# Four adaLN units per layer summed by TensorE in the router's span, branch and out products in another order without GpSimd, and the overfull-expert branch in the last expert pair

## The chip, the cores and the metric

The kernel runs on one core of a Trainium2 chip. The metric is the device time of one execution in microseconds (us). Besides TensorE (PE; its weight loads are listed as PEld) the core has VectorE (DVE), ScalarE (ACT), GpSimd (POOL) and SyncE (SP), which here issues the loads of weights; 16 DMA engines carry them.

## The reference

Two layers work on 256 tokens of width 1024. Six vectors per layer ("sections") come from one product with the conditioning vector c (adaLN): shift, scale and gate for the mixer and for the experts.

```python
c_act = jax.nn.silu(c)
for l in range(DEPTH):                              # 2
    mod = c_act @ ada_w[l] + ada_b[l]               # ada_w[l]: 1024 x 6144
    sh1, sc1, g1 = ...                              # sections 0, 1, 2
    sh2, sc2, g2 = ...                              # sections 3, 4, 5
    h = rmsnorm(x, norm1_g[l]) * (1.0 + sc1) + sh1
    x = x + g1 * token_mix(h, ...)
    h = rmsnorm(x, norm2_g[l]) * (1.0 + sc2) + sh2
    x = x + g2 * grouped_moe(h, w_router, router_bias, w_gate[l], w_up[l], w_down[l])
return rmsnorm(x, final_g)

# token_mix, its end:
    o_a = rmsnorm(o_a, hg_norm_g) * jax.nn.silu(hgate)
    merged = sigmoid(gates_a) * (o_a @ w_br_a) + sigmoid(gates_b) * (o_b @ w_br_b)
    return merged @ w_out

# grouped_moe: 16 experts of width 512, the best 2 of one group of 4 for each token
    he = jax.nn.silu(t @ w_gate[e]) * (t @ w_up[e])
    y = y + combine[:, e:e + 1] * (he @ w_down[e])
```

## The kernel before

Activations stand transposed (128 channels by 256 tokens, 8 such blocks). Every product of the mixer splits its fp32 weights into a high and a low part: `wunit` casts a 128x512 block on ACT and subtracts on DVE (both L409), into a ring of four buffers, and PE then makes 12 matmuls of 128x256 from it (L551). The sections of the input projection come in the order lat, qf, vg, ga, gb; then attention and the recurrence; then the branch products ("br", w_br_a and w_br_b) and the product with w_out ("out"). In `br` there are four steps i, each with a pair of output blocks: two units with the attention result `ob` make `gb`, two with the recurrence's result (`oah`, `oal`, which lie in buffers attn and vm) make `ga`, each multiplied on DVE (L909); GpSimd (for i < 3) then adds them to `m` (L913) and subtracts for the low part `hB` of the merged value, ACT casts the high part `hA`. `out` then takes its units one block of 128 columns after another, each over both halves of `hA` and `hB`.

`chain()` normalises the heads of the recurrence: four reciprocals (L884), two scaled copies (L886), a product with the output gate on GpSimd (L889) and a split with the subtraction on GpSimd. It is run a step at a time by `tick()`, which `wunit` calls: every unit advances each generator in the list `aside` by one.

adaLN: the first two sections of layer 0 are summed by PE at the start (`ada_sum`, L356: 8 matmuls of 128x256 with 32 columns of weights for a unit, a quarter of a section; the profile shows each as two; ACT copies the bank, L360; `ada_finish` adds four row groups by matmuls with one column and the bias on DVE). All other sections are summed by a custom reduction on DVE, two instructions of 128x1024 for a unit (`ada_steps`, L376, shown as CUSTOM_DVE_ANT_0). These are spread by `tick()` too, one instruction in 2 units of the mixer in layer 0, in 3 in layer 1: layer 0 has six sections (24 units), layer 1 four (16 units). What is left when the heads are done is run after the gates (layer 1) and after `br` (`while aside: tick()`).

The experts: tokens are sorted into 64 slots per expert by one-hot matrices. `moe()` makes the router's products (L979, L181), chooses on DVE (up to `selb`, L1026), ranks by a matmul with the triangle `tri`, gathers the tokens of four experts (L181, then L1103 and L1105), and runs the experts in eight pairs: gate and up (L1112), `he` (L1178), four transposes (L1187), a copy `heT` (L1189), down (L1121), and a scatter-add. `overflow()` holds a conditional block (`tc.If`, L1144, on a count that every engine's sequencer loads, L1141) for experts with over 64 tokens; it is placed between the first gather and the first pair. In these runs the block is not entered.

The order on each engine is the program's. SP's queue issues all weight loads (`fetch`, L190) in one order, each waiting until its buffer is free. The buffers A0, A1, B0, B1, C0, C1, x0, x1 hold 2 MB, r0, r1, hA, hB, n8, o9 1 MB, vm and attn 0.5 MB; several hold an activation in one phase and a weight in another. `early` and `late` load pieces of the first pairs' weights into activation buffers that have become free, `latest` one more (n8) behind the conditional block.

Of the kernel before, what the change touches and what calls it, by code (L numbers as in the profile page):

```python
# [19 lines left out]
P = 128  # L20
# [47 lines left out]
N_MSK = P * (len(LEVELS) + 2)  # L68
SECTIONS = ("qf", "vg", "ga", "gb", "br", "out")
# [31 lines left out]
def _lay_out(v):  # L101
# [31 lines left out]
    ada = _rows(w[:1, :, :2 * D]).reshape(P, J, 8, QD)  # L133
    ada = np.moveaxis(ada, 2, 0).reshape(2, 4, P, QUART)
# [21 lines left out]
def trunk(ctx: ExitStack, tc: tile.TileContext, x, pos, vec_in, msk_in, lat_in, wb, wq_in, wkv_in, ada_in, adat_in, crow_in, we,  # L156
# [72 lines left out]
    ada_at = {0: [(0, 2), (0, 3), (0, 4), (0, 5), (1, 0), (1, 1)], 1: [(1, 2), (1, 3), (1, 4), (1, 5)]}  # L229
# [6 lines left out]
    def issue():  # L236
        while todo and not todo[0]:
            todo.pop(0)
        for n, part in enumerate(todo[:2]):
            while part:  # L240
                key = part[0]
                if key[0] == "sec":
                    tags = ("A0", "A1", "B0") if key[2] in ("lat", "qf") else ("A0", "A1")
                elif key[1] > layer[0] or n and todo[0] and (todo[0][0][0] == "moe" or todo[0][0][2] in ("lat", "qf")):
                    break
                else:
                    tags = ("B0", "B1", "C0", "C1", "x0", "x1") + (() if n and todo[0] else ("A0", "A1"))
                s = [t for t in tags if t in free and t not in blocked]
                if not s:
                    break  # L250
                part.pop(0)
                if key[0] == "sec":
                    _, l, name, h = key
                    fetch(key, s[0], lat_in[l, h] if name == "lat" else wb[l, SECTIONS.index(name), h],
                          cuts=4 if key == ("sec", 1, "lat", 0) else 1)
                    if key == ("sec", 0, "lat", 0):
                        first_load(2)
                else:
                    _, l, p, i, h = key
                    fetch(key[:4], s[0], we[l, p, i][:, h * HALF:(h + 1) * HALF], h * HALF,  # L260
                          cuts=(1 if p < E // 2 - 1 else 4 if (i, h) in ((1, 1), (2, 1)) else 2))
# [9 lines left out]
    def early(l):  # L271
        at = HALF
        for t in ("vm", "attn", "r1"):
# [3 lines left out]

    def late(l):
        free.add("hA")
        fetch(("moe", l, 1, 1), "hA", we[l, 1, 1][:, HALF:HALF + QUART], HALF)  # L280

    def latest(l):
        at = HALF + QUART
        fetch(("moe", l, 1, 1), "n8", we[l, 1, 1][:, at:at + QUART], at)
# [8 lines left out]
    again, used_up = {}, {}  # L293
# [58 lines left out]
    def ada_sum(l, s, q, w, part):  # L352
        b = bank()
        for j in range(J):
            g = 32 * (j % 4)
            op = pe.matmul(b[g:g + 32, :QD], ca[:, j:j + 1].to_broadcast([P, 32]), w[:, j * QD:(j + 1) * QD],  # L356
                           start=j < 4, stop=j >= 4, tile_position=(0, g))
            if j == 0:
                tc.keep_in_program_order(op)
        ac.copy(part, b[:, :QD])  # L360
# [118 lines left out]
    def mixer(l, hs, after):  # L479
# [130 lines left out]
        aside.append(ada_steps(ada_at[l], 6, 2 if l == 0 else 3))  # L610
# [250 lines left out]
        disown("x0")  # L861
# [15 lines left out]
        def chain():  # L877
            yield
            for i, b in enumerate(ob_):
# [14 lines left out]
        aside.append(chain())  # L894
# [5 lines left out]
        while len(aside) > 1 or aside and l:  # L900
            tick()
        disown("C0")
        mg = [solo(t, [P, J, T], F32R) for t in ("hA", "hB")]
        w = section(l, "br")
        for i in range(4):
            js = slice(2 * i, 2 * i + 2)
            for g, ks, o in ((gb, 4, (ob[:, 0], ob[:, 1])), (ga, 0, (oah, oal))):
                b = pair(w, 256 * i, o, ks=(ks,), kx=ks)
                ve.scalar_tensor_tensor(g[:, js, :], g[:, js, :], 1.0, b.rearrange("p (h t) -> p h t", h=2),  # L909
                                        op0=ALU.add, op1=ALU.mult)  # L910
            m = t2("m")
            eng = gp if i < 3 else ve
            eng.tensor_tensor(m, gb[:, js, :], ga[:, js, :], ALU.add)  # L913
            split(mg[0][:, js, :], mg[1][:, js, :], m, eng)
            if i % 2:
                done("sec", l, "br", i // 2)
        disown("C1")
        while aside:
            tick()
        early(l)  # L920
# [5 lines left out]
        for i in range(4):  # L926
            b = pair(w, 256 * i, mg)
            for h in range(2):
                j = 2 * i + h
                ve.scalar_tensor_tensor(xT[:, j, :], b[:, h * T:(h + 1) * T], hg1[:, j:j + 1],  # L930
                                        xT[:, j, :], op0=ALU.mult, op1=ALU.add)
            if i % 2:
                done("sec", l, "out", i // 2)
            if i in (1, 2):
                next(after)
        disown("x1")
        late(l)

    def moe(l):
# [28 lines left out]
        for i in range(2):  # L968
# [15 lines left out]
            if i == 0:  # L984
                yield
        ve.tensor_reduce(rt, ssq, axis=AX.X, op=ALU.add)
# [12 lines left out]
        for (t, i), b in bx.items():  # L999
            ac.activation(hth[:, t, 4 * i:4 * i + 4, :], b.rearrange("p (q d) -> p q d", q=4), AF.Copy, scale=rv[:, t:t + 1])  # L1000
        bi = sm(TE, "bi")
# [159 lines left out]
        gather(oh, (2, 3))  # L1161
        weights(0, oh)
        overflow()
        latest(l)
        for p in range(E // 2):
# [6 lines left out]
            if last:  # L1172
                scatter(p - 1)
# [15 lines left out]
            ac.copy(heT, b.rearrange("p (j s) -> p j s", j=FJ))  # L1189
            if p and not last:  # L1190
# [121 lines left out]
```

## Time and profile before

| | |
|---|---|
| median of 3 runs | 987.47 us (983.97, 988.82, 987.47) |
| profiled execution | 983.23 us, span 981.4 us, mean granted clock 0.963 |
| busy: PE, DVE, ACT, POOL | 893.2 us (91%), 524.3 (53%), 340.5 (35%), 51.9 (5%) |
| DMA | 316.71 MB, mean 323 GB/s |
| L551, matmuls with hA (1312 of them) | 242.8 us, 16.1 us idle before them |
| layer 0: mixer to the end of the out product | 0 to 274 us |
| layer 0: router and experts | 274 to 506 us |
| layer 1: mixer | 506 to 737 us |
| layer 1: router and experts, then the final norm | 737 to 981.4 us |

The profile lists one execution. Busy time is that of an engine's own work; an idle time stands with the instruction that ended it, and with what released it ("<-"). PEclk is the granted share of TensorE's full clock. The stages in the last rows are read off the timeline of PE.

### The profile page before, as it was taken

How to read it: one execution, taken by the hardware profiler on the slowest of the kernel's cores; microseconds unless marked ns; L12 is line 12 of the kernel's file. 1: busy time of each engine (PE TensorE's matmuls, PEld its weight loads, DVE VectorE, ACT ScalarE, POOL GpSimd, SP SyncE). 2: the span in 40 equal slices, each digit the busy share in tenths (PEclk: the TensorE clock that was granted, in tenths of full speed). 3: DMA queues.
4: the chain of work that ended last, by engine and by line, in shares of the span. 5: the costliest groups of instructions: out<-in, count | busy, mean ns of one | idle time of the engine just before them, and what ended most of it. 6: DMA issues, size and time to landing. Idle time of an engine off the chain costs nothing. (4 is left out here: it accounts for less than half of the span.)

```text
span 981.4 us, 14762 instructions
## 1 busy us (share of the span) xinstructions
PE 893.2 (91%) x5958; PEld 635.6 (65%) x5958; DVE 524.3 (53%) x972; ACT 340.5 (35%) x632; POOL 51.9 (5%) x42
## 2 busy tenths in 40 slices
PE   5899999967969999999979999997895999999995
PEld 3688999957953535344349989997894353535333
DVE  4469898998540322222256968979854122322224
ACT  5465564524340212111146646554434111111103
POOL 0001100023000000000000020002300000000002
PEclk9899999998879999999999999999997999999998
DMA  9996665977659899999978626686585979999991
GB/s 362 430 378 225 234 224 217 380 307 315 253 210 381 344 384 430 434 427 429 422 299 329 271 91 248 253 326 250 224 348 200 398 306 433 429 429 433 426 386 43
DMA packets 35648, 316.71 MB, mean 323 GB/s; under 512 B 3952, under 2 KB 4208, under 8 KB 13808
## 3 DMA queue, kind: packets, MB, share of 16 engines
q1 hardware_dynamic: 35568, 315.64, 79.5%
q8 instruction: 50, 0.82, 0.3%
q14 instruction: 30, 0.25, 0.1%
HBM read 314.58 MB, written 1.05 MB: 322 GB/s over the span
## 5 line engine op out<-in xcount | busy, mean ns | idle before, releaser
L551 PE MATMUL bank<-hA,x 128*128 128x256 f32 x1312 | 242.8, 286 | 16.1 <-ACT x L409 8.8
L551 PEld LDWEIGHTS bank<-hA,x 128*128 128x128 f32 x1312 | 205.5, 192 | 20.3 <-DVE x L409 9.9
L551 PE MATMUL bank<-hB,x 128*128 128x256 f32 x656 | 184.7, 282 | 0.0
L551 PEld LDWEIGHTS bank<-hB,x 128*128 128x128 f32 x656 | 125.9, 192 | 0.2
L1178 DVE TENSOR_TENSOR he<-bank,sg 128x512 f32<-128x512 f32 x16 | 11.1, 692 | 141.8 <-PE bank L1112 113.4
L1137 DVE SCALAR_TENSOR_TENSOR xT<-bank,mod,xT 128x256 f32<-128x256 f32 x128 | 52.9, 478 | 58.1 <-PE bank L181 58.1
L1197 DVE SCALAR_TENSOR_TENSOR r<-bank,small,r 128x512 fp32r<-128x512 f32 (+1 forms) x36 | 24.7, 691 | 95.1 <-ACT r L1196 95.1
L1196 ACT ACTIVATE r<-bank,small 128x512 fp32r<-128x512 f32 (+1 forms) x36 | 22.8, 638 | 103.4 <-PE bank L1121 103.2
L1112 PE MATMUL bank<-moe_0B,o 128*64 128x512 f32 x192 | 47.6, 645 | 6.0 <-DVEq L1144 3.4
L1170 ACT ACTIVATE sg<-bank 128x512 f32<-128x512 f32 x16 | 9.6, 597 | 111.6 <-PE bank L1112 111.6
L1112 PE MATMUL bank<-moe_1x,o 128*64 128x512 f32 x192 | 43.4, 593 | 0.0
L1103 ACT ACTIVATE o<-bank,mod,acol 128x256 f32<-128x256 f32 x32 | 18.1, 564 | 58.5 <-DVE o L1105 55.0
L1189 ACT COPY heT<-bank 128x512 f32<-128x512 f32 x16 | 9.4, 588 | 83.4 <-PE bank L1187 83.4
L1112 PEld LDWEIGHTS bank<-moe_0B,o 128*64 128x64 f32 x192 | 15.2, 148 | 33.1 <-issue 32.6
L1112 PE MATMUL bank<-moe_1C,o 128*64 128x512 f32 x160 | 36.1, 592 | 0.0
L1105 DVE TENSOR_SCALAR o<-bank,acol,mod 128x256 f32<-128x256 f32 x32 | 17.4, 544 | 31.1 <-PE bank L181 28.2
L551 PE MATMUL bank<-o,x 128*128 128x256 f32 x192 | 28.1, 304 | 6.4 <-ACT x L409 3.4
L551 PE MATMUL bank<-attn,x 128*128 128x256 f32 x128 | 26.6, 300 | 6.4 <-DVE x L409 5.0
L1121 PE MATMUL bank<-moe_2C,heT 128*64 128x512 f32 (+1 forms) x160 | 29.2, 511 | 2.7 <-ACT heT L1189 2.7
L697 POOL TENSOR_TENSOR x<-ra,rbt 32x512 f32<-32x512 f32 x8 | 12.9, 1613 | 354.0 <-DVE rbt L693 353.5
L551 PEld LDWEIGHTS bank<-o,x 128*128 128x128 f32 x192 | 26.4, 212 | 7.2 <-ACT x L409 3.8
L1112 PEld LDWEIGHTS bank<-moe_1x,o 128*64 128x64 f32 x192 | 13.9, 137 | 26.2 <-issue 25.9
(298 smaller groups left out, 1719.6 us busy)
## 6 DMA issues: line engine op xcount, KB each, us to landing
moe_0B<-in_we SPq DMA_DIRECT2D x8, 2048.0 KB, 9.5
moe_1x<-in_we SPq DMA_DIRECT2D x8, 2048.0 KB, 13.0
moe_0A<-in_we SPq DMA_DIRECT2D x8, 2048.0 KB, 12.5
moe_1C<-in_we SPq DMA_DIRECT2D x6, 2048.0 KB, 12.3
moe_2C<-in_we SPq DMA_DIRECT2D x6, 2048.0 KB, 14.0
moe_1A<-in_we SPq DMA_DIRECT2D x6, 2048.0 KB, 18.1
moe_2A<-in_we SPq DMA_DIRECT2D x6, 2048.0 KB, 15.4
moe_2x<-in_we SPq DMA_DIRECT2D x6, 2048.0 KB, 20.1
```

The costliest lines, as they stand in the source:

```text
L551: pe.matmul(o, a[:, k, :], b[:, k0 + k, :], start=first and k == 0 and q == 0, stop=last and k == 3 and q == 2)
L697: gp.tensor_tensor(qT[64:96, i::4, :], ra[q4], rbt[q4], ALU.add)
L1103: ac.activation(o, bq, AF.Identity, bias=sh2[:, j:j + 1], scale=acol[:, j:j + 1])
L1105: ve.tensor_scalar(o, bq, acol[:, j:j + 1], sh2[:, j:j + 1], op0=ALU.mult, op1=ALU.add)
L1112: pe.matmul(b[64 * q:64 * q + 64, :], x(j, q), w[:, o:o + 512], start=(j == 0), stop=(j == J - 1), tile_position=(0, 64 * q))
L1121: pe.matmul(b[64 * q:64 * q + 64].rearrange("p (c n) -> p c n", n=256)[:, c % 2:c % 2 + n], x[:, j, 64 * q:64 * q + 64], _ap(w[:, o:o + 25 ...
L1137: ve.scalar_tensor_tensor(xT[:, j, :], b[:, q * T:(q + 1) * T], g2[:, j:j + 1], xT[:, j, :], op0=ALU.mult, op1=ALU.add)
L1170: ac.activation(sg, bg.rearrange("s (j f) -> s j f", j=FJ), AF.Silu)
L1178: ve.tensor_tensor(he, bu.rearrange("s (j f) -> s j f", j=FJ), sg, ALU.mult)
L1189: ac.copy(heT, b.rearrange("p (j s) -> p j s", j=FJ))
L1196: ac.activation(yv[:, 0, d], b[:, s], AF.Copy, scale=wc)
L1197: ve.scalar_tensor_tensor(yv[:, 1, d], b[:, s], wc, yv[:, 0, d], op0=ALU.mult, op1=ALU.subtract)
```

## The change

1. One adaLN section per layer (layer 1's section 1 during layer 0, and layer 1's section 5 during layer 1; `ADA_ROWS`), four units each, goes from DVE to PE. The 4 MB of it are fetched in two halves of 2 MB into x0 (after attention) and C0 (after the heads' chain), instead of four of 1 MB into r0 and r1. PE sums them into two banks between the router's products and the ranking, ACT copies both banks, and 8 one-column matmuls and one DVE addition finish them after the gather.
2. GpSimd is taken out of `chain()`, `m` and the split of it: DVE does them. The heads' chain is drained before `br`, no adaLN step runs within `br`; the rest is put back into `aside` for `out`.
3. `br` goes gb, gb, ga, ga for two steps i at a time. `out` goes through the first half of `hA`, `hB` for four blocks in four banks, then the second half.
4. `early` loads vm and attn where it did, r1 after `out`; `late` loads hA and n8, and `latest` is gone.
5. The conditional block moves to the last pair of experts, between the copy `heT` and the down product. `hold` keeps the next layer's section loads, all but the first, behind it.

```diff
-    def early(l):
-        at = HALF
-        for t in ("vm", "attn", "r1"):
+    def early(l, *tags):
+        at = HALF if len(tags) > 1 else HALF + QUART
+        for t in tags:
...
+    def ada_fetch(l, h, tag):
+        blocked.discard(tag)
+        fetch(("adp", l, h), tag, ada_in[2 + l, 2 * h:2 * h + 2].rearrange("q p n -> p q n"))
...
-    ada_at = {0: [(0, 2), (0, 3), (0, 4), (0, 5), (1, 0), (1, 1)], 1: [(1, 2), (1, 3), (1, 4), (1, 5)]}
+    ada_at = {0: [(0, 2), (0, 3), (0, 4), (0, 5), (1, 0)], 1: [(1, 2), (1, 3), (1, 4)]}
...
+                if key[0] in hold and key[3:] and key[2:] != ("lat", 0):
+                    break
...
-        disown("x0")
+        ada_fetch(l, 0, "x0")
...
-                gp.tensor_tensor(o, o, hg[:, 2 * i:2 * i + 2, :], ALU.mult)
+                ve.tensor_tensor(o, o, hg[:, 2 * i:2 * i + 2, :], ALU.mult)
                 yield
-                split(oah[:, 2 * i:2 * i + 2, :], oal[:, 2 * i:2 * i + 2, :], o, gp)
+                split(oah[:, 2 * i:2 * i + 2, :], oal[:, 2 * i:2 * i + 2, :], o)
...
-        while len(aside) > 1 or aside and l:
-            tick()
-        disown("C0")
+        for _ in heads:
+            pass
+        aside.clear()
+        ada_fetch(l, 1, "C0")
...
-        for i in range(4):
-            js = slice(2 * i, 2 * i + 2)
+        for i0 in (0, 2):
             for g, ks, o in ((gb, 4, (ob[:, 0], ob[:, 1])), (ga, 0, (oah, oal))):
-                b = pair(w, 256 * i, o, ks=(ks,), kx=ks)
...
-            eng = gp if i < 3 else ve
+                for i in (i0, i0 + 1):
+                    js = slice(2 * i, 2 * i + 2)
+                    b = pair(w, 256 * i, o, ks=(ks,), kx=ks)
...
-        for i in range(4):
-            b = pair(w, 256 * i, mg)
...
+        for i0 in (0, 4):
+            bs = [bank() for _ in range(4)]
+            for k in (0, 4):
+                for j, b in enumerate(bs):
+                    product(wunit(w(k, (i0 + j) * P)), mg, k, b[:, :T], k == 0, k == 4)
...
+        parts = []
+        for h in range(2):
+            b = bank()
+            for q in range(2):
+                ada_rows(b[:, q * QD:(q + 1) * QD], take("adp", l, h)[:, q * QUART:(q + 1) * QUART])
+            done("adp", l, h)
+            parts.append(b)
         ve.tensor_reduce(rt, ssq, axis=AX.X, op=ALU.add)
...
+        b, (al, asec) = bank(), ADA_ROWS[2 + l]
+        for j in range(J):
+            mm(b[:, j:j + 1], parts[j // 4][:, j % 4 * P:(j % 4 + 1) * P], v_("four"), True, True)
+        ve.tensor_add(mod[al][:, asec, :], b[:, :J], v_("adab", (al * 6 + asec) * J, J))
         weights(0, oh)
-        overflow()
-        latest(l)
...
             if last:
+                hold.add("sec")
                 scatter(p - 1)
...
             ac.copy(heT, b.rearrange("p (j s) -> p j s", j=FJ))
+            if last:
+                overflow()
+                hold.clear()
+                issue()
```

Where the change moves instructions, line numbers of the changed file are larger: L376 is L384 there, L409 is L417, L909 and L913 are L921 and L925, L1112 is L1136.

DVE at the end of layer 0's branch products, before (the L376 rows are the adaLN reductions, the L409 row the low part of the merged value that the out product reads):

```order
L909 SCALAR_TENSOR_TENSOR C_21_175<-C_21_175,bank_2206 128x512
L913 TENSOR_TENSOR m_2236<-C_21_175 128x512
L376 ISA ada_1_3r_203_2057,mod_91<-ada_1_3r_203_2057,crow,vec 128x1024
L376 ISA mod_91 128x1
L376 ISA ada_1_3r_203_2057,mod_91<-ada_1_3r_203_2057,crow,vec 128x1024
L376 ISA mod_91 128x1
L409 TENSOR_TENSOR hB_1970<-m_2236,hA_1969 128x512
```

and after (L417 on x_25_180 are subtractions for weight units, here already those of the out product):

```order
L921 SCALAR_TENSOR_TENSOR C_21_175<-C_21_175,bank_2154 128x512
L417 TENSOR_TENSOR x_25_180<-sec_out_0A_202_2092,x_25_180 128x512
L925 TENSOR_TENSOR m_2184<-C_21_175 128x512
L417 TENSOR_TENSOR x_25_180<-sec_out_0A_202_2092,x_25_180 128x512
L384 ISA ada_0_3r_189_1870,mod_91<-ada_0_3r_189_1870,crow,vec 128x1024
L384 ISA mod_91 128x1
L417 TENSOR_TENSOR hB_1963<-m_2184,hA_1962 128x512
L921 SCALAR_TENSOR_TENSOR C_21_175<-C_21_175,bank_2188 128x512
```

In place of a product `m` and two whole units of adaLN ahead of the low part, the weight units of the out product stand between them, and one adaLN instruction at a time.

PE in layer 0's router, before (bank_2451 takes the router's logits, `selb` is the choice of experts that DVE makes):

```order
L979 MATMUL bank_2539<-vec,xT 128x128 x2
L181 MATMUL bank_2451<-wrs_2257,xT 128x16
L181 LDWEIGHTS tri
L181 MATMUL bank_2592<-selb_2590,tri 128x16
```

and after (`adp` are the two halves of the adaLN section, `ca` the conditioning vector):

```order
L993 MATMUL bank_2529<-vec,xT 128x128 x2
L360 MATMUL bank_2554<-adp_0x_175_1674,ca 32x256 x15
L360 MATMUL bank_2573<-adp_1C_193_1960,ca 32x256 x16
L182 LDWEIGHTS tri
L182 MATMUL bank_2624<-selb_2622,tri 128x16
```

The 32 adaLN matmuls of the section (8 to a unit) now stand between the router's products and the ranking.

PE around the conditional block of layer 0, before (the last matmuls of `weights`, ahead of the first pair):

```order
L181 MATMUL bank_2652<-oh_2599,r_246_2573 128x256 x4
L181 MATMUL bank_2663<-sr_2614,oh_2599 128x2 x8
L1141 TENSOR_LOAD cmaxi_2612
L1144 COMPARE_AND_BRANCH
```

and after (the last pair's up product, its four transposes, and the block):

```order
L1136 MATMUL bank_3714<-moe_7_1A_392_3570,o_260_2650 64x512 x8
L1214 MATMUL bank_3732<-vec,he_3683 128x128 x4
L1165 TENSOR_LOAD cmaxi_2644
L1168 COMPARE_AND_BRANCH
```

The block has gone from between the gather and the first gate product to between the transposes and the last down product.

More of the change, by code (lines that the diff above doesn't have):

```diff
@@ L276, in early @@
             at += size[t]
+    def ada_fetch(l, h, tag):
+        blocked.discard(tag)
+        fetch(("adp", l, h), tag, ada_in[2 + l, 2 * h:2 * h + 2].rearrange("q p n -> p q n"))
     def late(l):
[L279 to L284, printed above, removed]
+        for n, t in enumerate(("hA", "n8")):
+            at = HALF + n * QUART
+            free.add(t)
+            fetch(("moe", l, 1, 1), t, we[l, 1, 1][:, at:at + QUART], at)
     def take(*key):
@@ L291, in done @@
         issue()
-    again, used_up = {}, {}
+    again, used_up, hold = {}, {}, set()
     def spent(l, p, i, j):
@@ L350, in trunk, with ada_rows @@
     mod = [one.tile([P, 6, J], F32, name=f"mod{l}") for l in range(DEPTH)]
-    def ada_sum(l, s, q, w, part):
-        b = bank()
+    def ada_rows(o, w):
         for j in range(J):
             g = 32 * (j % 4)
-            op = pe.matmul(b[g:g + 32, :QD], ca[:, j:j + 1].to_broadcast([P, 32]), w[:, j * QD:(j + 1) * QD],
+            op = pe.matmul(o[g:g + 32], ca[:, j:j + 1].to_broadcast([P, 32]), w[:, j * QD:(j + 1) * QD],
                            start=j < 4, stop=j >= 4, tile_position=(0, g))
@@ L359, in ada_sum @@
                 tc.keep_in_program_order(op)
+    def ada_sum(l, s, q, w, part):
+        b = bank()
+        ada_rows(b[:, :QD], w)
         ac.copy(part, b[:, :QD])
@@ L609, in mixer @@
             masks()
-        aside.append(ada_steps(ada_at[l], 6, 2 if l == 0 else 3))
+        steps = ada_steps(ada_at[l], 6, 2 if l == 0 else 3)
+        aside.append(steps)
         for i in range(5):
@@ L925, in mixer @@
         next(after)
-        for i in range(4):
-            b = pair(w, 256 * i, mg)
[L928 to L935, printed above, removed]
+        aside.append(steps)
+        for i0 in (0, 4):
[3 more added lines that the diff above has]
+                    product(wunit(w(k, (i0 + j) * P)), mg, k, b[:, :T], k == 0, k == 4)
+                    if k:
+                        ve.scalar_tensor_tensor(xT[:, i0 + j, :], b[:, :T], hg1[:, i0 + j:i0 + j + 1],
+                                                xT[:, i0 + j, :], op0=ALU.mult, op1=ALU.add)
+                if bool(i0) != bool(k):
+                    next(after)
+            done("sec", l, "out", i0 // 4)
+        while aside:
+            tick()
         disown("x1")
+        early(l, "r1")
         late(l)
@@ L1000, in moe @@
             ac.activation(hth[:, t, 4 * i:4 * i + 4, :], b.rearrange("p (q d) -> p q d", q=4), AF.Copy, scale=rv[:, t:t + 1])
+        for h in range(2):
+            b, parts[h] = parts[h], t2("part", [P, 2 * QD])
+            ac.copy(parts[h], b)
         bi = sm(TE, "bi")
```

27 lines of the change are left out of this document (14 added, 13 removed).

## The prediction

> **What bounds the kernel.** I read the stages first: the span cut where PE's work changes, with the busy time of PE, DVE, ACT, POOL, the granted clock and the DMA share (columns: stretch, its length, busy time with instruction counts of PE, PEld, DVE, ACT, POOL, PEclk, DMA share, GB/s).
>
> ```profile
> 206.00:238.00 32.00, 25.80 (x192) 24.80 (x192) 28.57 (x42) 12.48 (x22) 11.99 (x8) 0.89 0.82 325
> 274.00:293.00 19.00, 9.93 (x75) 9.73 (x73) 11.00 (x39) 9.93 (x22) 0.00 (x0) 0.69 0.45 175
> 293.00:506.00 213.00, 207.37 (x1108) 92.55 (x1108) 52.78 (x113) 32.91 (x56) 0.00 (x0) 0.99 0.94 393
> ```
>
> PE carries the kernel (207.37 of 213 us in the experts), and what it loses lies at two places per layer. One is the end of the mixer, where DVE is busy for 28.57 of 32 us; the other is the router, where PE works 9.93 of 19 us. So I cut finer there (PE alone: stretch, length, PE busy, PEclk, DMA share, GB/s), and asked whom PE waited for from 208.6 to 247 us.
>
> ```profile
> 198.00:247.00 49.00, 32.94 (x240) 0.86 0.79 306
> 247.00:275.00 28.00, 28.00 (x235) 0.94 0.68 270
> 671.00:697.00 26.00, 17.11 (x123) 0.93 0.62 243
> 697.00:737.00 40.00, 40.00 (x336) 0.96 0.82 316
> 198.00:208.60 10.60, 6.05 (x45) 1.00 0.58 193
> PE bank L551 <- ACT x L409: 5.0, 1, 5.0
> PE bank L551 <- DVE x L409: 4.9, 2, 2.8
> PE bank L551 <- POOL vm L409: 1.5, 1, 1.5
> ```
>
> In layer 0 PE stands idle for 49.00 − 32.94 = 16.1 us between 198 and 247 us, and its clock is below full there and until 275 us. Taking the missing share of the clock as lost PE time: 0.14 x 32.94 + 0.06 x 28.00 = 6.3 us. Together 22.4 us. In layer 1: 26.00 − 17.11 = 8.9 us idle, and 0.07 x 17.11 + 0.04 x 40.00 = 2.8 us, together 11.7. The waits are for ACT and DVE in L409, the making of weight units, and the timeline of DVE (start, length, engine, line) tells why they are late.
>
> ```profile
> 217.27 2.49 DVE L409 TENSOR_TENSOR x<-sec_br_0A,x 128x512 fp32r<-128x512 f32 x4
> 236.27 1.72 DVE L376 CUSTOM_DVE_ANT_0 ada_2r<-ada_2r,crow,vec 128x1024 f32<-128x1024 f32 x1
> 237.92 2.27 DVE L376 CUSTOM_DVE_ANT_0 ada_2r<-ada_2r,crow,vec 128x1024 f32<-128x1024 f32 x1
> 241.51 1.28 DVE L376 CUSTOM_DVE_ANT_0 ada_3r<-ada_3r,crow,vec 128x1024 f32<-128x1024 f32 x1
> 242.71 1.28 DVE L376 CUSTOM_DVE_ANT_0 ada_3r<-ada_3r,crow,vec 128x1024 f32<-128x1024 f32 x1
> 243.92 0.69 DVE L409 TENSOR_TENSOR hB<-m,hA 128x512 fp32r<-128x512 f32 x1
> 242.82 0.58 PE L551 MATMUL bank<-hA,x 128*128 128x256 f32 x1 [5.03 <-ACT x L409]
> 224.00:238.00 14.00, 13.79 (x122) 1.00 0.68 274
> 196.57 2.16 POOL L409 TENSOR_TENSOR vm<-o,attn 128x512 fp32r<-128x512 f32 x1 [0.73 <-ACT attn L409]
> ```
>
> From 236.27 to 243.92 DVE runs four adaLN reductions and the last `m`; the low part `hB` waits behind them, and PE starts `out` after 5.03 us idle. A reduction takes 1.2 us start to start alone (241.51, 242.71) and 2.27 us at 237.92, where GpSimd works beside it: the DVE work of this stretch is long in part because of GpSimd, which itself takes 2.16 us for one subtraction.
>
> The clock: the gaps of PE and the matmuls behind them.
>
> ```profile
> 245.80:250.60 4.80, 4.80 (x22) 0.50 0.96 393
> 250.60:255.40 4.80, 4.80 (x43) 1.00 0.90 373
> 292.98 6.33 PE L1112 MATMUL bank<-moe_0B,o 128*64 128x512 f32 x16 [2.56 <-PEq L1144]
> 293.00:298.00 5.00, 5.00 (x12) 0.50 0.81 296
> 755.57 0.96 PE L1112 MATMUL bank<-moe_0B,o 128*64 128x512 f32 x2 [3.44 <-DVEq L1144]
> 755.60:759.20 3.60, 3.60 (x10) 0.53 0.75 241
> ```
>
> Behind a gap of 2.56 us or more the granted clock is 0.50 for about 5 us, and 22 matmuls pass where 43 pass at full clock. [...]
>
> **The change, part by part.**
>
> (1) Mixer's end, layer 0. Removed from DVE: eight reductions of the section that goes to PE (8 x 1.2 = 9.6 us alone, up to 2.27 each), and the others from `br`. Added: in `br` three `m` and three subtractions, in the chain two products and two subtractions, at 0.62 us each by the x4 row (2.49 / 4). Per step i of `br` DVE then has 4 units, 2 products L909, `m` and the low part: 8 x 0.62 = 5.0 us. PE needs 4 units x 12 matmuls x 13.79/122 = 0.113 us, 5.4 us. So PE sets the pace, narrowly. `out` begins with the first halves of `hA`, `hB`, so the last low part is no longer in its way. GpSimd's operations of about 2 us leave the path, and DVE reductions lose their neighbour. What stays is the gate phase, where PE is idle for 10.60 − 6.05 = 4.55 us before `br`, and the chain's four operations that are new on DVE there, 4 x 0.62 = 2.5 us: 7.0 us. Gain 22.4 − 7.0 = 15.4, I take 15. Bounds: 10, if half of the clock loss and some 2 us of idle come back; 18, if the gate phase gains as well.
>
> (2) The same in layer 1. By the counts, the 24 reductions there are over before `br` (24 x 3 = 72 ticks, plus the start). Of the 11.7 us I leave 1.7 for draining the chain (up to four operations of 0.4 to 0.9 us before the first units of `br`). Gain 10; bounds 7 and 11.7.
>
> (3) Router. PE's rows there:
>
> ```profile
> 744.79 0.20 PE L181 MATMUL bank<-selb,tri 128*128 128x16 bf16 x2 [5.61 <-DVE selb L1026]
> 19.30 1.07 PE L356 MATMUL bank<-first,ca 128*32 128x256 f32 x16
> L181 PE MATMUL bank<-vec,part x32: 164/250/271, 18.8 to 44.3; 128*128 128x1 f32 x32
> L360 ACT COPY part<-bank x8: 347/372/385, 18.3 to 42.3; 128x256 f32<-128x256 f32 x8
> 751.18 0.95 PE L181 MATMUL bank<-sr,oh 128*128 128x2 f32 x8
> ```
>
> Four units at up to 1.07 us are 4.3 us, inside the 5.6 us in which PE waits for DVE's choice: nothing, if their weights are there. They also shorten the gap to about 1.3 us. Two ACT copies of twice the size (0.37 to 0.74 each) lie in the same stretch: nothing, or 1.5 us if the gather's evictions, ACT's next work, come late by as much. The finish, 8 one-column matmuls, shows as 16 (8 units at the start with 2 each made 32 rows). By the 751.18 row, 0.95 / 8, that is 1.9 us on PE's path; the 250 ns median of the same instruction, were they not overlapped, gives 4.0 as the upper end. I take 1.9 a layer, within the next term.
>
> (4) The conditional block leaves the place before the experts. Both gaps go (2.56 and 3.44), and with them the half clock behind them: 0.50 x 5.00 = 2.5 and 0.47 x 3.60 = 1.7. Layer 0: 2.56 + 2.5 = 5.1; layer 1: 3.44 + 1.7 = 5.1; each less 1.9 from (3) is 3.2, 6.4 in all. Bounds: 2.2, with 4.0 for the finish, and 10.2, if it hides. The n8 piece no longer waits for the block.
>
> (5) The block at its new place, between the transposes and the last down product:
>
> ```profile
> L1144 PEldq COMPARE_BRANCH  x2: 3768/3780/3792, 288.9 to 750.7; - x2
> L1141 PEldq TENSOR_LOAD <-cmaxi x2: 315/402/490, 288.3 to 750.3; - x2
> L1144 DVEq COMPARE_BRANCH  x2: 63/68/72, 291.1 to 752.6; - x2
> 955.90 0.66 PE L1187 MATMUL bank<-vec,he 128*128 128x128 f32 x4 [0.86 <-DVE he L1178]
> 957.23 1.08 PE L1121 MATMUL bank<-moe_2C,heT 128*64 128x256 f32 x8 [0.67 <-ACT heT L1189]
> ```
>
> PE's sequencer loads the count at 288.3 and the next matmul starts at 292.98: 4.7 us; in layer 1, 750.3 to 755.57, 5.3. Here it can load when the transposes are issued, between 955.90 and 956.56, so the down product starts near 961.0 in place of 957.23: +3.8. That gap is over 4 us, so the clock falls for about 5 us of the down and scatter work: +2.1 (between 1.7 and 2.5 of (4)). Both layers: 2 x 5.9 = +11.8. Bounds: +1, if the sequencer's 3.8 us overlap the wait for `heT` and the clock holds; +16, if layer 1's 5.3 us hold for both and the next layer's loads, started later, cost 1.5 us each. Behind the block PE has only the down product, DVE and ACT only what reads it, and SP the next layer's sections; lat's first half is let through ahead, and the experts' weights are all issued by then.
>
> (6) Transfers. The same bytes, but x0 and C0 now take 4.2 MB of adaLN weights late in the mixer, and two 2 MB pieces of the experts' only after the router's sums.
>
> ```profile
> 806.00:955.00 149.00, 147.29 (x766) 1.00 1.00 422
> 752.00:755.60 3.60, 0.16 (x4) 1.00 0.03 9
> ```
>
> The experts run with the DMA engines full (1.00) and PE at 147.29 of 149 us: they are nearly even, with little PE idle yet. Against a loss speaks that the mixer's end has spare bandwidth (0.58 to 0.79), and from 752 to 755.6 the queue does nothing at all (9 GB/s), because it too stands at the block. I take nothing; bounds 0 and +9.9 us a layer (4.2 MB at 422 GB/s).
>
> **The sum**: −15 −10 −6.4 + 11.8 = −19.6 us on the profiled execution's 983.2 us (span 981.4 and 1.8 around it), 963.6. The profiled one is the fastest of the four times shown; their mean is 985.9, 2.6 above. So 966 us as a median (987.5 before).
>
> **The rivals.**
>
> A, the forecast: 966 us.
>
> B, the block costs next to nothing at its new place, since the sequencer may run ahead while `heT` is made: without term (5) −31.4, 983.2 + 2.6 − 31.4 = 954 us. Against it: PE's next matmul followed the branch in both layers. [...]
>
> C, DVE paces `br`: its operations there take not 0.62 but the mean of the groups below, 0.79 us (between 777 and 809). Then a step takes 8 x 0.79 = 6.3 in place of 5.4 us, 4 x 0.9 x 2 = +7: 973 us.
>
> ```profile
> L409 DVE TENSOR_TENSOR x<-sec_br_0A,x 128x512 fp32r<-128x512 f32 x16 | 12.4, 809 | 1.2 <-ACT x L409 1.2
> L409 DVE TENSOR_TENSOR x<-sec_br_1A,x 128x512 fp32r<-128x512 f32 x16 | 12.0, 777 | 1.6 <-ACT x L409 1.5
> ```
>
> These means hold the slow ones beside GpSimd, which speaks against it.
>
> D, slower: DVE becomes the bound of `br` and its gaps halve the clock. The place is the low part in DVE's queue: it waits there for ACT's cast of `hA`, as GpSimd did (0.73 us in the row of 196.57), and the weight units behind it wait too. A step then takes 6.3 + 0.73 = 7.0 us, 1.6 over PE's; four steps lose 6.4 us and the tail 1.5 a layer, and if gaps of over 2.5 us arise at each second step, the clock is at half for most of `br`: 21.8 us of work at 0.113, with half of it slow, +10.9. That is 18.8 a layer, 37.6 against the 19.6 saved: +18, 1004 us. It decides against the change from about 10 us a layer, which needs the gaps; without them (7.9 a layer) it ends at 982. For it speaks only that DVE's margin is 0.4 us a step.
>
> E, the experts run short of weights: up to 2 x 9.9 us given back, 986 us; half of it 976. A full DMA share beside a nearly full PE speaks for it, the idle bandwidth just before against it.
>
> **How the numbers follow.** Chances: A 0.58, B 0.13, C 0.14, D 0.07, E 0.08. Half a per cent, 4.9 us, is about what a measurement of this kernel can tell from no change. A, B and C are all faster by more, and of E two parts in four: 0.89; the same 0.04 (the rest of E, a part of D); slower 0.07. The range for 8 in 10: A's own is 955 to 976 by the bounds of the terms; taking in B's 954 and the unequal times of one kernel (984 to 989) it is 948 to 979.
>
> **What would show it.** In `br` of the changed kernel no gap of PE beyond 1 us and a clock of 1.00 if (1) and (2) hold; reductions all at about 1.2 us start to start. In the router the adaLN matmuls ahead of a gap of 1 to 2 us, and the first expert product at full clock straight after the gather. In the last pair a gap of about 4 us ahead of the down product and half clock behind it; if that gap is 1 us, B. If the mixer's end keeps more than 10 us idle per layer, C or D; if PE waits for DMA in the first two pairs, E. What would make it wrong above all is the size of (1): the gate phase of layer 0 keeps its reductions, and a late unit there could shift more than the 7 us that I leave.

## The result and the profile after

The changed kernel takes 958.47 us (median of 4 runs, 953.63 to 961.92) against 985.72 us before (4 runs, 983.67 to 988.82): ratio 0.974, 95% interval 0.971 to 0.977. The profiled execution took 959.52 us, its span is 957.8 us (before 981.4), its mean granted clock 0.976 (before 0.963). The forecast was 966 us within 948 to 979. The time lies inside, but its terms lie less well: the mixers' ends gave 6.8 us more than forecast and the block's new place cost 5 less, while the router, which was to give 6.4, gave nothing. That these misses partly cancel in the sum is luck.

To see where the time went I cut both traces at the same five points in each layer: the first weight cast of the last gate section, the router's first transpose, the first expert matmul, the last of the four transposes in the last pair, and the matmul behind these. Lengths in us, worked out from the starts in the two timelines and rounded:

| stage | before, L0 / L1 | after, L0 / L1 | difference | forecast |
|---|---|---|---|---|
| last gate, `br`, `out` | 96.3 / 87.3 | 79.0 / 72.8 | −17.3, −14.5 | −15, −10 |
| router and gather, to the first expert matmul | 26.7 / 26.9 | 26.7 / 27.3 | 0.0, +0.4 | −6.4 together, |
| experts, to the last transposes | 201.7 / 200.7 | 200.9 / 201.0 | −0.8, +0.3 | with the row above |
| last transposes to the next matmul | 0.9 / 0.9 | 4.2 / 3.8 | +3.3, +2.8 | +11.8 together, |
| from there to the next layer's last gate, or to the end of the span | 145.8 / 24.2 | 145.2 / 25.8 | −0.6, +1.6 | with the row above |

With +1.2 at the start, which the change doesn't touch, they add up to −23.6 us, the difference of the two spans.

The mixer's end, PE alone (stretch, its length, PE busy, PEclk, DMA share, GB/s), before:

```profile
198.00:266.20 68.20, 52.14 (x392) 0.87 0.76 300
671.00:728.70 57.70, 48.80 (x382) 0.94 0.75 291
```

and after, with what PE still waited for from 199 to 258 us, and one row of the reductions on DVE:

```profile
199.20:250.10 50.90, 47.93 (x398) 1.00 0.78 301
656.80:700.00 43.20, 43.20 (x381) 1.00 0.82 317
PE bank L559 <- DVE x L417: 2.0, 3, 1.1
PE bank L559 <- ACT x L417: 1.5, 1, 1.5
L384 DVE CUSTOM_DVE_ANT_0 ada_3r<-ada_3r,crow,vec x16: 1272/1280/1285, 87.6 to 649.8; 128x1024 f32<-128x1024 f32 x16
```

In layer 1 the same work (381 and 382 rows) fills its 43.20 us without a gap and at full clock; in layer 0, 3.0 us of idle are left, all in the gates and at the first units of `br`. No reduction takes over 1.292 us any more.

The router of layer 0 and the first experts, timeline of PE and clock:

```profile
267.14 0.19 PE L182 MATMUL bank<-selb,tri 128*128 128x16 bf16 x2 [2.17 <-DVE selb L1050]
274.15 1.84 PE L182 MATMUL bank<-vec,part 128*128 128x1 f32 x16
275.85 1.03 PE L182 MATMUL bank<-sr,oh 128*128 128x2 f32 x8
276.81 8.73 PE L1136 MATMUL bank<-moe_0B,o 128*64 128x512 f32 x32
276.80:280.20 3.40, 3.40 (x9) 0.51 1.00 429
280.20:283.60 3.40, 3.40 (x18) 1.00 0.94 395
```

The gap ahead of the ranking has shrunk from 5.6 to 2.17 us and the gap ahead of the experts is gone, and still the first experts run at 0.51 of the clock, 9 matmuls where 18 fit.

The last pair of both layers, and what stands behind the block in layer 0:

```profile
482.00 5.12 PE L1145 MATMUL bank<-moe_2A,heT 128*64 128x256 f32 x32 [3.97 <-PEq L1168]
931.98 5.36 PE L1145 MATMUL bank<-moe_2A,heT 128*64 128x256 f32 x32 [3.49 <-PEq L1168]
L1168 PEldq COMPARE_BRANCH  x2: 3307/3458/3608, 478.0 to 928.2; - x2
481.60:485.00 3.40, 3.00 (x15) 0.51 0.69 213
```

A gap of 3.97 and 3.49 us, as forecast, and half clock for one stretch of 3.4 us, not for 5.

### The profile page after: what moved, and what is told of

Its sections match the earlier page's. It is cut to its first block, busy times and chain, and to the rows that moved or that the text cites. A ratio compares the mean times of both kernels' runs of the same rounds, so it can differ in the third digit from the quotient of the medians.

```text
span 957.8 us, 15041 instructions
## 1 busy us (share of the span) xinstructions
PE 898.9 (94%) x6118; PEld 637.5 (67%) x6118; DVE 503.7 (53%) x962; ACT 349.1 (36%) x640; POOL 20.2 (2%) x22
## 5 line engine op out<-in xcount | busy, mean ns | idle before, releaser
L1136 PE MATMUL bank<-moe_0B,o 128*64 128x512 f32 x192 | 46.5, 633 | 0.0
L1136 PE MATMUL bank<-moe_1C,o 128*64 128x512 f32 x192 | 43.3, 593 | 0.0
L1145 PE MATMUL bank<-moe_2A,heT 128*64 128x512 f32 (+1 forms) x160 | 32.3, 557 | 8.8 <-PEq L1168 7.5
L1136 PE MATMUL bank<-moe_1A,o 128*64 128x512 f32 x160 | 36.1, 593 | 0.0
L1136 PEld LDWEIGHTS bank<-moe_0B,o 128*64 128x64 f32 x192 | 14.0, 145 | 27.1 <-issue 26.6
L1136 PEld LDWEIGHTS bank<-moe_1C,o 128*64 128x64 f32 x192 | 13.6, 137 | 26.6 <-issue 25.7
L1145 PE MATMUL bank<-moe_2x,heT 128*64 128x512 f32 (+1 forms) x160 | 29.6, 512 | 0.0
L1145 PEld LDWEIGHTS bank<-moe_2A,heT 128*64 128x64 f32 x160 | 13.4, 155 | 24.2 <-issue 20.3
L182 PE MATMUL bank<-C 128*128 128x64 f32 (+1 forms) x240 | 29.2, 272 | 0.0
L1136 PE MATMUL bank<-moe_0x,o 128*64 128x512 f32 x128 | 28.6, 594 | 0.0
## 6 DMA issues: line engine op xcount, KB each, us to landing
moe_1C<-in_we SPq DMA_DIRECT2D x8, 2048.0 KB, 14.5
```

What stands on the lines that cost most here:

```text
L182: pe.matmul(o, l, r, start=start, stop=stop)
L1136: pe.matmul(b[64 * q:64 * q + 64, :], x(j, q), w[:, o:o + 512], start=(j == 0), stop=(j == J - 1), tile_position=(0, 64 * q))
L1145: pe.matmul(b[64 * q:64 * q + 64].rearrange("p (c n) -> p c n", n=256)[:, c % 2:c % 2 + n], x[:, j, 64 * q:64 * q + 64], _ap(w[:, o:o + 25 ...
```

## The experiments

All twelve ratios below are to the kernel before, timed on the same chip beside it. The changed kernel stands at 0.974 (0.971 to 0.977).

**The block at its old place.** The edit, in the changed kernel (with it `hold.add` goes, and `late` loads hA alone):

```diff
         weights(0, oh)
+        overflow()
+        latest(l)
         for p in range(E // 2):
...
-            if last:
-                overflow()
-                hold.clear()
-                issue()
```

> The changed kernel with the conditional block back between the first gather and the first expert pair (the n8 load behind it again, no holding back of the next layer's sections); all else as changed. Theory 1 (from the marks of the two traces: the move cost +3.3 and +2.8 us of gap at the new place and about 1.5 us of half clock each, and took away gaps of 2.56 and 3.44 us while half clock stayed at the experts' start): the move is worth nothing, 956 to 961 us against 958.5 for the change. Rival 1a, the prediction's terms without the finish (gaps and half clock of 10.2 us return, 11.8 us go): 957, with the experts' first matmuls at half clock for 5 us in layer 0. Rival 1b: the move was a gain, since the block also held up the weight queue ahead of the experts: 964 us or more.

963.39 us, ratio 0.980 (0.977 to 0.984): slower than the change by 5 to 6 us (the two intervals just touch), more than theory 1 allowed, just short of rival 1b. The trace shows a cause that neither had. The block at the old place now costs more than it did before the change:

```profile
282.38 7.89 PE L1138 MATMUL bank<-moe_0B,o 128*64 128x512 f32 x24 [4.95 <-PEq L1170]
L1170 PEldq COMPARE_BRANCH  x2: 5945/6010/6076, 275.9 to 729.6; - x2
278.00:280.00 2.00, 0.00 (x0) 0.50 0.94 401
```

while the kernel before had, at the same place in its program:

```profile
288.90:291.00 2.10, 1.51 (x15) 1.00 0.06 12
291.00:293.00 2.00, 0.03 (x2) 0.64 0.03 8
```

PE's branch lasts 6.0 us in place of 3.8, at a DMA share of 0.94 in its middle in place of 0.03 to 0.06. Before, the queue of weights had run dry at the block; in the changed kernel it has not. That became theory 4.

**No block at all** (the call and `hold.add` deleted):

> The changed kernel without the conditional block at all (experts with over 64 tokens would lose the tokens beyond; there are none in these inputs) and without holding the next layer's sections back. Theory 1: the block in the last pair costs what the marks show, 3.3 + 2.8 us of gap and about 1.5 us of half clock a layer in part absorbed behind it, 7 us in all: 951 to 952. Rival, the prediction's term in full (5.9 us a layer): 947.

952.22 us, ratio 0.968 (0.964 to 0.973), and the gaps at the block go, 3.3 and 2.8 us: theory 1. The block in the last pair costs about 6 us in both layers together, half of the 11.8 forecast.

**The finish of the adaLN section later** (the eight one-column matmuls and the addition go behind the first pair's `he`):

```diff
-        b, (al, asec) = bank(), ADA_ROWS[2 + l]
...
             ve.tensor_tensor(he, bu.rearrange("s (j f) -> s j f", j=FJ), sg, ALU.mult)
+            if p == 0:
+                b, (al, asec) = bank(), ADA_ROWS[2 + l]
+                for j in range(J):
+                    mm(b[:, j:j + 1], parts[j // 4][:, j % 4 * P:(j % 4 + 1) * P], v_("four"), True, True)
+                ve.tensor_add(mod[al][:, asec, :], b[:, :J], v_("adab", (al * 6 + asec) * J, J))
```

> The changed kernel with the eight one-column matmuls that finish the adaLN section (16 in the profile, 1.7 us) moved from ahead of the experts into the first pair, between its up product and its transposes, where PE waits 0.87 us for DVE. Theory 2: these narrow matmuls both take 1.7 us and bring the half clock that the trace shows at the experts' start (3.4 us windows at 276.8 and 727.3), so that about 3.4 us a layer go, less 0.8 for what the gap does not hide: 953 us. Rival 2a: the half clock there comes from the idle 2.17 us ahead of the ranking and stays; only the hidden part goes, 0.9 us a layer: 956.7. Rival 2b: late weights take it back: 958.

956.73 us, ratio 0.974 (0.971 to 0.978). In time that is rival 2a. In the trace it is theory 2 at its own place:

```profile
268.84 1.86 PE L182 MATMUL bank<-oh,r 128*128 128x256 f32 x7 [0.23 <-DVE r L1075]
273.98 7.09 PE L1136 MATMUL bank<-moe_0B,o 128*64 128x512 f32 x32
274.00:277.40 3.40, 3.40 (x17) 1.00 1.01 424
287.87 1.95 PE L182 MATMUL bank<-vec,part 128*128 128x1 f32 x16
476.90:483.70 6.80, 5.24 (x26) 0.50 0.58 206
```

The first experts run at full clock though the gap ahead of the ranking is the same 2.17 us, so the half clock hung on the narrow matmuls. But these alone do not decide it, as the next run shows. Router and experts are 2.6 us (layer 0) and 3.2 us (layer 1) shorter. Some 3.6 us of it are lost again behind the block, where half clock now lasts 6.8 us in place of 3.4 with a gap of the same length. In this trace the low stretches begin at multiples of 3.41 us of each other (268.7, 476.9, 497.4, 719.2 and 927.5), which would explain it if what a gap costs depends on how it lies on that grid.

**GpSimd back** in the chain and in `m` and its low part:

```diff
-                ve.tensor_tensor(o, o, hg[:, 2 * i:2 * i + 2, :], ALU.mult)
+                gp.tensor_tensor(o, o, hg[:, 2 * i:2 * i + 2, :], ALU.mult)
...
-                        split(mg[0][:, js, :], mg[1][:, js, :], m)
+                        split(mg[0][:, js, :], mg[1][:, js, :], m, eng)     # eng = gp if i < 3 else ve
```

> The changed kernel with GpSimd back in the heads' chain (product and low part) and in the branch products' sum and low part for the first three steps; order and adaLN as changed. Theory 3 (what was gained beyond the forecast at the mixers' ends, 30.7 in place of 25 us, is mostly DVE freed of adaLN there, GpSimd's own share is small): up to 962 us. Rival 3: GpSimd beside DVE is the main cost (reductions of 2.27 us, units of up to 1.7 us beside it): 10 us or more return, 968 us or above.

962.47 us, ratio 0.981 (0.977 to 0.985). Theory 3, at its upper edge: the mixers' ends grow by 2.7 and 1.5 us. This run also corrects the reading of the last one. Its 24 rows of narrow matmuls (the finish and the eight with two columns) stand where they stand in the change, and its first experts still run at full clock in both layers:

```profile
280.00:283.40 3.40, 3.40 (x17) 1.00 1.02 439
730.00:733.40 3.40, 3.40 (x17) 1.00 1.04 439
```

I set the rows against the grid of each execution, read off the starts of its low stretches. Seven of the runs, the change among them, have all 24 rows directly ahead of the block or the experts, and six of them have no block there: twelve starts of experts. In eight the clock was halved, and there 2.2 to 2.7 us of the rows lay in one stretch of 3.41 us; in four it was not (both layers here, layer 0 with the old order of the branch products, layer 1 without holding back), and there it was at most 2.0 us. In the twelve starts of the six runs with eight of these rows there, 0.95 us of them, it never was. So by these 24 starts the finish ahead of the experts costs a half clock or not by the luck of the grid; its move takes the risk away.

**The section back on DVE** (`ADA_ROWS` and `ada_at` as in the kernel before for this, no `ada_fetch`, no `parts`, no finish):

> The changed kernel with the fourth adaLN section per layer back on DVE (20 to 24 and 12 to 16 units, fetched into r0 and r1), none of it on TensorE; adaLN still kept out of the branch products, the rest in the out product. Theory 3: what counted at the mixers' ends is that the reductions left the branch products and their neighbours; in the out product DVE has 16 splits of 0.6, 8 products of 0.48 and 8 reductions of 1.2 us, 23 us, beside PE's 21.8, so the section itself costs DVE little there, while the router gets 0.9 + 1.7 us a layer back: 955 to 961. Rival: the section on TensorE is the gain, DVE falls behind again: 965 us or more.

963.68 us, ratio 0.980 (0.975 to 0.985), between the theory and its rival. The marks say that this is not the section's price: up to the last pair's transposes layer 0 is 0.2 us longer and layer 1 2.9 us shorter than in the change. What is lost is lost at the block, where a load of the next layer had been issued ahead of it, the branch lasted 6.06 us in layer 0, and PE stood for 8.08 us, the last 2 of them for DVE, which passed its own branch late. Two further runs (below) take this up.

**The old order of the out product.**

> The changed kernel with the out product in its old order (each block of columns over both halves of hA and hB). Theory 3: PE then waits at the start of out for the last cast and low part, which it reached 5.03 us late before; with no adaLN in between it is 2 to 3 us a layer and a half clock window of 1.7 in one or both: 963 to 966. Rival: with DVE no longer behind, the order is worth nothing: 957 to 960.

963.23 us, ratio 0.978 (0.973 to 0.982): the time of theory 3 and not its reason. PE waits 0.2 us for `hB`, and that only in layer 0; the first router transpose comes 1.8 us later in each layer (the last 0.9, no more than the spread between runs, see below), and 1.2 and 0.7 us of that are a wait for the router's scaled weights, which this order asks for sooner:

```profile
PE bank L182 <- DVE wrs L970: 1.2, 1, 1.2
PE bank L559 <- DVE hB L417: 0.2, 1, 0.2
```

**The old order of the branch products.**

> The changed kernel with the branch products in their old order (gb, gb, ga, ga for one step at a time, so two pairs of units between the merged sums). Theory 3: PE sets the pace there either way (5.4 against 5.0 us a step), worth under 1.5 us a layer: 958 to 961. Rival: the heads' chain is late for ga, and the old order stands two units closer to it: 963 us or more, with a gap of PE at the first ga unit.

958.43 us, ratio 0.974 (0.970 to 0.979): theory 3, worth nothing measurable (0.0 and +1.0 us at the mixers' ends).

**No holding back of the next layer's loads** (`hold.add("sec")` deleted): the test of theory 4.

> The changed kernel without holding the next layer's section loads behind the block: one more load (1.4 MB) is issued ahead of it in layer 0; layer 1 is the same. Theory 4 (from the run with the block before the experts: PE's compare-and-branch lasts 5.9 to 6.1 us with the DMA engines full beside it, 3.8 us with them empty, 3.3 to 3.6 in the change, because what comes behind the branch is fetched by the same engines): with 1.4 MB more in flight, layer 0's branch lasts 1.5 to 2.5 us longer than its 3.3, layer 1's the same; the next layer's first weights come 3 us earlier, which PE doesn't need: 959 to 961. Rival 4a: the branch's length has nothing to do with the DMA engines, it stays at 3.3: 958. Rival 4b: the earlier load is worth more than the branch: 955 to 957.

963.51 us, ratio 0.980 (0.975 to 0.986). The branch of layer 0, with the DMA engines at 1.07 beside it from 478.2 to 481.2 us, against 0.47 in the change:

```profile
L1168 PEldq COMPARE_BRANCH  x2: 3447/4648/5848, 477.5 to 930.4; - x2
478.20:481.20 3.00, 0.00 (x0) 1.00 1.07 432
```

and the change in the same stretch:

```profile
478.20:481.20 3.00, 0.00 (x0) 1.00 0.47 181
```

The branch lasted 5.85 us in layer 0 against 3.61 in the change, 2.2 us longer, as theory 4 had it. (Its 3.3 was layer 1's branch: of the two in the change the one of 478.0 lasts 3.61 us, the one of 928.2 lasts 3.31.) In layer 1, where nothing was changed, it is 3.45 against 3.31. Rivals 4a and 4b fall. The whole ran 2.5 us slower than expected; half clock behind the block was 6.8 us in both layers.

**adaLN within the branch products** (section on DVE, `aside.clear()` deleted, `hold` set ahead of the last pair's gate product):

> As the run with the section back on DVE, but with adaLN steps allowed within the branch products, as before (no clearing; holding back of the next layer's loads set one product earlier, so that none of them is in flight at the block). GpSimd stays out, branch and out products stay in the new order. Theory 3: the reductions within the branch products are the largest part of the 30.7 us, since undoing GpSimd's part, the out order and the branch order one at a time gave back only 5, 3.6 and 1 us at the mixers' ends: 12 to 18 us there against the run without them, 968 to 975 us. Rival: with GpSimd gone and the new order, DVE has room, the three parts each needed the others: 957 to 962.

965.07 us, ratio 0.981 (0.978 to 0.983): halfway between the rival and theory 3. PE waits 6.4 us for DVE in 8 places of layer 0. Against the next run, which differs in this alone, the router's first transpose comes 11.6 and 5.5 us later, 17 us, as theory 3 had it. But in layer 0 the first transpose is a poor mark: it stands among the `out` units and came early in the next run, whose last transpose did not. To the router's last transpose the difference is 6.9 and 5.5 us, and to the first expert matmul, where reductions that were only put off come out, 5.3 and 5.6 us: 11 us in all.

**The section on DVE with the loads held back sooner.**

> The run with the section back on DVE again, with the holding back of the next layer's loads set one product earlier: there one of them (1.4 MB) was issued ahead of the block, PE's branch in layer 0 lasted 6.1 us and the half clock 10 us. Theory 5: without that the section on TensorE is worth nothing by itself (2.9 us lost in layer 1's stages, 0.2 gained in layer 0's): 955 to 958. Rival: it is a gain of its own, 960 or more.

961.58 us, ratio 0.976 (0.973 to 0.978). This is the rival's number, and again not for the rival's reason. Up to the last transposes both layers are shorter than in the change (2.2 us in layer 0, 3.1 in layer 1). At the block of layer 0 PE's own branch took 3.88 us, but PE waited 7.8: DVE came to its branch late, since a subtraction for the next layer stood ahead of it and waited for ACT's cast, which ACT began at 478.2 us, after the copy `heT` and a table load (1.28 us each in the change). DVE's next instruction started 4.22 us after that subtraction had ended, and PE went on with it.

```profile
478.85 0.69 DVE L417 TENSOR_TENSOR x<-sec_lat_0A,x 128x512 fp32r<-128x512 f32 x1 [3.48 <-ACT x L417]
483.76 1.90 DVE L417 TENSOR_TENSOR x<-sec_lat_0A,x 128x512 fp32r<-128x512 f32 x3 [4.22 <-DVEq L1158]
PE bank L1135 <- DVEq L1158: 7.8, 1, 7.8
```

**The section on DVE without the block**, to be compared with the run without the block above:

> The change without the conditional block (tokens of experts over 64 would be lost; none here) and with the fourth adaLN section per layer on DVE: to be set against the run without the block whose section is on TensorE (952.2 us, ratio to the kernel before 0.968). Both runs with the section on DVE so far were disturbed at the block (6.1 us of branch, then a DVE that passed its branch 3.9 us late); their marks up to the last pair's transposes were 2.8 and 3.5 us a layer shorter or equal in the router and the experts. Theory 5: without the block to disturb it the section on DVE is no slower than on TensorE, 946 to 951 us (ratio 0.960 to 0.966). Rival: the section on TensorE is a gain, 955 or more (0.970 or more), by DVE late in out and router. In between, 951 to 955, it is worth nothing either way.

948.82 us (5 runs), ratio 0.963 (0.961 to 0.965), against 0.968 (0.964 to 0.973) with the section on TensorE. Theory 5: the section on TensorE is no gain, and by the medians 3 us of loss, with intervals that just touch. By the marks the section on DVE is 0.5 us ahead up to layer 0's last router transpose; then it loses 1.1, since PE waits 7.9 us for the choice of experts (two reductions stand in DVE's queue there); the two stretches of experts are 1.6 and 1.0 us shorter, since they start at full clock, and layer 1's mixer and router together 2.1.

```profile
PE bank L182 <- DVE selb L1040: 7.9, 1, 7.9
```

**The block one step earlier**, between `he` and the transposes, with the late finish, and `hold` set ahead of the last gate product:

```diff
+            if last:
+                overflow()
+                hold.clear()
+                issue()
             b = bank()
             for j in range(FJ):
                 pe.transpose(b[:, j * P:(j + 1) * P], he[:, j, :], ident)
```

> The changed kernel with the finish of the adaLN section in the first pair, and the conditional block one step earlier in the last pair, between the up product and the transposes, so that PE's sequencer can reach it while the up product's matmuls still run (in the kernel before it loaded the count 2 us ahead of its last matmul), and the 0.87 us wait for DVE falls into the same gap. Theory 4: a gap of 2 to 3 us in place of 4.0 and 0.87: 952 to 955 against 956.7 for the later finish alone. Rival: the weights still in flight at that time lengthen the branch to 6 us, as ahead of the experts, which eats it: 957 to 959.

955.40 us, ratio 0.969 (0.966 to 0.972): the fastest here of the kernels that keep the block. Both were right in part. The gaps are 2.41 and 3.58 us, with the 0.87 us wait inside them, and the branch is long:

```profile
477.89 0.63 PE L1220 MATMUL bank<-vec,he 128*128 128x128 f32 x4 [2.41 <-PEq L1168]
926.82 0.83 PE L1220 MATMUL bank<-vec,he 128*128 128x128 f32 x4 [3.58 <-DVEq L1168]
L1168 PEldq COMPARE_BRANCH  x2: 5199/5570/5942, 471.6 to 919.2; - x2
474.00:476.00 2.00, 1.48 (x8) 1.00 1.01 400
```

It begins at 471.6, ahead of 3.9 us of matmuls that PE already has, so most of its 5.9 us is hidden. Against the later finish alone (0.974, 0.971 to 0.978) the intervals overlap slightly, and the profiled spans are 0.8 us apart (954.7 and 955.5): whether it is faster than that one is not shown.

## Why the prediction was right, and where it was not

The sign and the bulk were right because the waits at the mixers' ends were read as DVE's; these stages gave 31.8 us, more than the whole gain of 23.6 us of span. The sum, −19.6 us on the profiled execution, came out 4 us from the measured one because misses of −6.8, +6.3 and −4.7 us went into it: that part is luck.

(1) and (2), forecast −15 and −10, came to −17.3 and −14.5. That `br` and `out` would be paced by PE (5.4 against 5.0 us a step) is right: from 210 us on PE is busy all the time there, at clock 1.00. The step that failed is the count of what was lost. In layer 1 I had 8.9 us idle plus 2.8 for the clock; the same matmuls now take 43.2 us in place of 57.7, 14.5 less: 8.9 idle and 48.80 − 43.20 = 5.6 us of slow work, twice the 2.8. In layer 0 the slow work was 52.14 − 47.93 = 4.2 us, two thirds of the 6.3. The missing share of the clock times the busy time is only a rough measure of what was slow: in layer 1 the clock was low for two stretches of 3.41 us, at most 3.4 us of loss, and where the other 2.2 us of slow work come from stays open. And what I left behind, 7.0 us in layer 0 and 1.7 in layer 1, measured 3.0 and 0: the four operations of the chain that moved to DVE brought no idle time of PE beyond what the gates had before (4.55 us in layer 0).

Which part brought it, by the marks to the router's last transpose, where the change gained 16.4 and 13.6 us: undone one at a time, GpSimd gives back 4.2 us over both layers, the out order 1.8, the branch order 1.0, adaLN within the branch products 12.4. The section on TensorE gives back nothing. The four runs that leave the mixers as they are (the block at its old place, no block, the finish later, no holding back) differ from the change by 0.0 to 1.9 us at the same mark, so only adaLN's share and a part of GpSimd's are clear of the spread between runs. More than 10 of the 30 us belong to no part undone alone. That the loads on DVE hurt more beside each other would explain it, but no run undid two of them at once, so this isn't shown.

(3) was right in its durations: the finish takes 1.7 us for the 1.9 forecast, and the sums of the section run inside the wait for DVE, which left a gap of 2.17 us and not 1.3. Missed was 0.9 us from the router's first transpose to its last. Two of the adaLN matmuls stand between the router's products and take 0.55 us of it; with the old out order, where none stands there, the distance is 10.1 us as before the change.

(4), forecast −6.4, came to about 0. The gaps of 2.56 and 3.44 went as forecast; what failed is the sentence that the half clock goes with them. It stayed because the matmuls with one and two columns ahead of the experts did not keep the clock up, as the grid lay in that execution; the run with the finish moved and the run with GpSimd back show it together. By the run with the block at the old place, though, the move is worth its 5 to 6 us: the block would not have cost 2.56 there but 4.95, with full DMA engines. I had priced it by the kernel before, whose queue had run dry at that point.

(5), forecast +11.8, is 7.1 by the marks and 6 by the run without the block. The gap was right (3.8 forecast, 3.3 and 2.8 above the old 0.9). The half clock was one stretch of 3.4 us, at most 1.7 us of loss a layer for the 2.1 forecast, and in layer 0 a wait of 0.98 us that stood behind the old last pair is gone.

(6), nothing, was right: no wait of PE for weights appears in the experts.

Rivals: B, C, D and E did not happen. Against B stand 3.3 to 6.1 us of compare-and-branch on PE's sequencer in all runs here that have the block. As to the clock, the low stretches lie on a grid of 3.41 us in these traces, and gaps of about 4 us cost 3.4 us of half clock in one execution (the change) and 6.8 in another (the finish later); that it is the grid which decides between the two fits these numbers and was not shown by itself.

Open: whether the section on DVE also wins with the block in place. Both such runs were disturbed at the block, one by a load and by DVE's order, one by DVE's order alone, and none without either was made. The new order of the loads (x0 and C0, `early`, `late`) was not undone by itself. That the spread of one kernel's runs (953.6 to 961.9 us) comes from the clock's grid is likely by the traces, but wasn't shown.

## What to carry to other kernels

When the engine that makes the weights ready is the one that falls behind, work that isn't urgent must leave the stretch where it falls behind; where it goes matters less than that it goes, and here the section given to TensorE brought nothing of its own. Price a wait at a place by the state that the changed kernel will have there: here a branch that cost 2.56 us beside an empty transfer queue (DMA share 0.05) cost 4.95 beside a full one (0.94 in its middle). And a stretch in which the timeline shows PE busy can still cost the clock: here it did when 2.2 us or more out of 3.41 were matmuls of one and two columns.

## What the runs showed of the hardware

- PE's compare-and-branch was long where the DMA engines were full. In 18 cases their mean share over the branch was 0.03 to 0.54, and it took 3.3 to 3.9 us, with no order among them (3.61 us at 0.45 and 3.31 at 0.03 in the change, 3.29 at 0.47 and 3.75 at 0.04 with GpSimd back). In six cases the share was 0.70 to 1.02, and it took 5.2 to 6.1 us: both layers of the old place in the changed kernel and of the block at the up product, layer 0 without holding back and with the section on DVE. The profile lists instruction packets among the DMA traffic (queue 8 moved 0.87 MB in the changed kernel and 0.79 in the run without the block), and three of them between start and end of PE's branch in each layer of the change, four in each of the kernel before. That PE waits for these packets there, as theory 4 has it, is the author's guess and was not shown.
- 24 rows of matmuls with one and two columns, 2.7 to 3.1 us almost without a gap, were followed by half clock in 8 of 12 places, those where 2.2 to 2.7 us of them fell into one stretch of the 3.41 us grid, and not in the 4 where at most 2.0 us did. With 16 of them gone it did not come in any of 12.
- In the profiled executions of the kernel before and of the change, half clock came in 23 stretches; they begin at multiples of 3.41 us of each other within each execution and last 3.41, 6.83 or 10.24 us (the last of each runs to the end of the span). Behind gaps of about 4 us at the block it lasted 3.4 us in the change and 6.8 us with the finish later.
